# Layer 0 of a two-layer decoder step: first projections by chunks of tokens, loads and gated units moved forward

## The chip, the cores and the metric

The kernel runs on one core of a Trainium2 chip. The time is that of the device, in microseconds (us), for one execution; a kernel's figure is the median of several executions. The engines are named as the profile names them: PE (TensorE matmuls; PEld its weight loads), DVE (VectorE), ACT (ScalarE), POOL (GpSimd), SP (SyncE, which here only issues DMAs). ACT and POOL issue DMAs too, in line with their other instructions.

## The reference, cut to what matters

One step of a decoder with two layers on 1024 prompt tokens and 8 x 4 sample tokens (1056 tokens in all, width 1024). The change lies in layer 0, which is a state-space layer with two branches:

```python
proj = rms_norm(x, g) @ w_in                 # [u 512 | z 1024 | xBC 2048 | dt 16]
u, z, xbc, dt_raw = split(proj)
ya, s5_h  = s5_mixer(u, ...)                 # diagonal scan, then a gate:
    # zg = einsum('bsgc,gce->bsge', y, glu_w) + glu_b;  out = zg[..., :16] * sigmoid(zg[..., 16:])
yb, ssd_h, conv_new = ssd_mixer(z, xbc, dt_raw, ...)
x += concat(ya, yb) @ w_out
```

`rms_norm` is `x * rsqrt(mean(x*x) + 1e-5) * g` for every token. Layer 1 (attention), the two MLPs and the last norm follow; they are not touched.

## The kernel before, in words

**Tiling.** Activations lie with 128 channels on the partitions and the 1056 tokens along a row, so a 1024-wide activation is 8 tiles `x`. The tokens go in three chunks of 352 (CH). Every f32 matmul is made of three: the operand is split into a high part (`xh`, `wh`: the rounded value) and a low part (`xl`: the rest), and `xh*wh`, `xl*wh`, `xh*wl` are summed in PSUM (L381, L382, L383, in `dense`). A unit of 128 output channels has 24 such matmuls a chunk. Its 1024 x 128 weights are loaded as `wr` and split by ACT (L312) and DVE (L313) in `w_split`.

**Norm.** For each chunk ACT squares the eight `x` tiles (L418), PE multiplies them by a 128 x 128 matrix of ones (L419), so that the sum over the channels stands on all 128 partitions, and DVE and ACT turn that 128 x 352 tile into the factor `rB`: TENSOR_SCALAR (L424), square root (L425), RECIPROCAL (L426). One row of the raw sum is stored in DRAM as `msx_d` (L422, L423), from which SP later loads `m1x` in another layout (L1275, L1276). DVE scales `x` by the norm's weight and `rB` (L431), ACT makes `xh` (L432), DVE `xl` (L433).

**Order.** The tile scheduler emits one in-order stream per engine. The program gives two lists, `main` (units) and `side` (the work of the mixers), and `merge` deals the one among the other. The first units of `main` are the four `u` units (0 to 3), whose output ACT copies out of PSUM into tiles `u` (L570) and stores as `u_d` (prompt) and `us_d` (samples); then come eight `z` units and the rest. `mm`, the PSUM tile of a chunk of a unit, has four buffers. The `u` tiles take slots that tiles `x` leave free. S5 works in four batches of 8 groups: `prep` steps form the batch's matrices (`R`, stored as `rt_d` and loaded back as `Tl`, L619 and L624), `load_u` loads `U` and `Us` from `u_d` and `us_d` (L684, L686, L687), and matmuls L698, L703 and L757 use them. `s5b` and `s5x` are two parameter tiles of S5, loaded by ACT (L438, L535).

Later in the layer four `ssd_group` lists run as `side` under `conv_unit` lists. Behind the third, each of the four gated units of S5 (`load_ya`) loads a 544 KB tile `ya` from `ya_d` (L1130), forms a weight tile `glu` on DVE (L1133), multiplies (L1141), applies the gate (ACT L1143, DVE L1145), and splits the result for the eight `oa` units, which project it.

**What is touched.** `w_split` (L305), the norm loop (L402 to L433), the order of the `u` units and of the S5 batches (L807 to L812), the loop over the groups (about L1113) and `load_ya` (L1128).

```python
T.matmul(p[:, :CH], C["ones"], sq[:, :CH], start=(k == 0), stop=(k == KD - 1))   # L419
for j in range(4):
    main += u_unit(j)                                                            # unit after unit
for j in range(4):
    load_ya(j)                                                                   # ahead of the oa units
```

Of the kernel before, what the change touches and what calls it, by code (L numbers as in the profile page):

```python
# [7 lines left out]
F32 = mybir.dt.float32  # L8
# [185 lines left out]
def _build(ctx, nc, tc, ins, outs, dbg):  # L194
# [100 lines left out]

    held = {U_IO + i for i in range(3)}
    AHEAD = 300

# [6 lines left out]
    def w_split(i, al=None):  # L305
        if i < len(units) and i not in hl and i not in held:
            w_load(i)
# [95 lines left out]
    msx_d = dp.tile([1, NT], F32, name="msx_d")  # L403
    xr = [slot(F32, "x") for _ in range(KD)]
    for c in range(3):
        cc = slice(c * CH, (c + 1) * CH)
        for k in range(KD):
            nc.sync.dma_start(xr[k][:, cc], ins["xT"][k][:, cc])
            if c == 0 and k == 3:
                w_load(0)  # L410
        if c == 0:
            w_load(1)
    for c in range(3):
        cc = slice(c * CH, (c + 1) * CH)
        p = px()
        for k in range(KD):
            sq = half(F32, "sq")
            S.activation(sq[:, :CH], xr[k][:, cc], AF.Square)  # L418
            T.matmul(p[:, :CH], C["ones"], sq[:, :CH], start=(k == 0), stop=(k == KD - 1))  # L419
        rB = half(F32, "rB")[:, :CH]  # L420
        ms = half(F32, "msx")
        V.tensor_copy(ms[0:1, :CH], p[0:1, :CH])  # L422
        nc.scalar.dma_start(msx_d[:, cc], ms[0:1, :CH])  # L423
        V.tensor_scalar(rB, p[:, :CH], 1.0 / D, EPS, op0=OP.mult, op1=OP.add)  # L424
        S.activation(rB, rB, AF.Sqrt)  # L425
        V.reciprocal(rB, rB)  # L426
        if c == 0:
            w_split(0)
        for k in range(KD):
# [378 lines left out]
    for j in range(4):  # L808
        pre, run = s5_batch(j)
        side += pre + run  # L810
    for j in range(4):
        main += u_unit(j)  # L812
    m1 = main
# [105 lines left out]
    def ssd_group(g):  # L919
# [178 lines left out]
        def fin(i):  # L1098
# [5 lines left out]
            if g < 3:  # L1104
# [6 lines left out]
                F(stage_b, 3), F(stage_c, 3), F(fin, 0), F(fin, 1)]  # L1111

    for f in dt_unit(12 + SPILL):  # L1113
        f()
    side = [dt_math]
    for g in range(4):
        main = []
        for k in range(4):
            if 4 * g + k >= SPILL:
                main += conv_unit(13 + 4 * g + k, 4 * g + k)  # L1120
        merge(main, side)
        side = ssd_group(g)
# [4 lines left out]
    def load_ya(j):  # L1127

        y, o = xslot(F32, "ya"), slot(F32, "yo")
        nc.sync.dma_start(y[:, :1088].rearrange("p (t n) -> p t n", t=8), ya_d[j])  # L1130
        w = half(F32, "glu")
# [29 lines left out]

    for j in range(4):
        load_ya(j)
    main = []
    for d in range(8):
# [1357 lines left out]
```

## Time and profile before

| | |
|---|---|
| median of 3 executions | 3127.24 us (3126.2 to 3130.1) |
| the profiled execution | 3129.79 us |
| its span in the trace | 3128.0 us |
| mean granted TensorE clock | 0.978 |
| DVE, ACT, POOL busy | 70%, 45%, 21% of the span |
| DMA traffic | 414.30 MB, mean 132 GB/s |

A view of waits lists who waited for whom, the longest total first. A timeline gives the instructions of an engine in order of time, those of one form in a row merged. Each engine works in order, so an instruction that waits holds up all that stand behind it in its stream.

### The profile page before, as it was taken

To read this page: it belongs to the slowest core of one execution; us is meant where nothing else is said; L and a number is where in the kernel's file an instruction comes from. 1 tells how busy PE (TensorE), PEld (TensorE's weight loads), DVE (VectorE), ACT (ScalarE), POOL (GpSimd) and SP (SyncE) were. 2 spreads that over 40 slices of the span, in tenths; PEclk is the share of its full clock that TensorE was granted. 3 is DMA by queue.
4 is the path that set the end of the run, shared out by engine and by line. 5 is a ranking of instruction groups with operands and counts; after the bars stand their busy time and mean duration, and the time that the engine had idled before them with its cause. 6 is when DMAs were issued, how large, how long until landed. Compare 5 with 4: busy or idle time off the path is not lost. (4 is left out here: it accounts for less than half of the span.)

```text
span 3128.0 us, 58908 instructions
## 1 busy us (share of the span) xinstructions
PE 2970.6 (95%) x22228; PEld 2798.3 (89%) x22228; DVE 2204.7 (70%) x4618; ACT 1412.5 (45%) x2920; POOL 662.9 (21%) x659
## 2 busy tenths in 40 slices
PE   7999998998999999999999989999989899999998
PEld 5999886898999999999999877777869899999998
DVE  5778787778777666866223778777766877757687
ACT  4224565433333344453226666656662433334343
POOL 0000000014222001241001343434332422200133
PEclk8999999998999999999999999999999899999999
DMA  5254444522444584676532121221134344467565
GB/s 187 88 136 136 106 138 118 160 104 96 143 142 146 176 287 130 202 248 192 155 89 76 18 66 45 39 56 38 27 83 137 106 149 144 141 218 244 150 222 159
DMA packets 301285, 414.30 MB, mean 132 GB/s; under 512 B 81012, under 2 KB 202071, under 8 KB 300935
## 3 DMA queue, kind: packets, MB, share of 16 engines
q1 hardware_dynamic: 264640, 340.87, 35.8%
q0 software_dynamic: 20800, 45.43, 5.8%
q10 hardware_dynamic: 15558, 24.22, 2.1%
q8 instruction: 175, 2.87, 0.4%
q14 instruction: 112, 0.91, 0.1%
HBM read 283.81 MB, written 118.18 MB: 129 GB/s over the span
## 5 line engine op out<-in xcount | busy, mean ns | idle before, releaser
L1514 PE MATMUL dn<-xb,sb 128*128 128x264 f32 x1664 | 473.0, 287 | 2.6 <-DVE xb L1427 2.6
L1515 PE MATMUL dn<-xb,sb 128*128 128x264 f32 x1664 | 468.2, 285 | 0.0
L1513 PE MATMUL dn<-xb,sb 128*128 128x264 f32 x1664 | 455.3, 286 | 12.9 <-ACT xb L1426 10.5
L1513 PEld LDWEIGHTS dn<-xb,sb 128*128 128x128 f32 x1664 | 306.8, 189 | 13.5 <-ACT xb L1426 10.9
L1514 PEld LDWEIGHTS dn<-xb,sb 128*128 128x128 f32 x1664 | 315.1, 189 | 3.5 <-DVE xb L1427 3.4
L1515 PEld LDWEIGHTS dn<-xb,sb 128*128 128x128 f32 x1664 | 316.0, 190 | 0.0
L1372 PE MATMUL A<-xw,sw 128*128 128x264 f32 x1024 | 294.8, 289 | 15.9 <-ACT sw L1326 8.5
L1373 PE MATMUL A<-xw,sw 128*128 128x264 f32 x1024 | 294.5, 288 | 3.4 <-DVE xw L1233 3.4
L1374 PE MATMUL A<-xw,sw 128*128 128x264 f32 x1024 | 293.5, 287 | 0.0
L2243 POOL TENSOR_SCALAR P<-P,s,gates 128x640 f32<-128x640 f32 (+7 forms) x256 | 212.2, 843 | 281.0 <-DVE s L2239 231.9
L381 PE MATMUL mm<-xh,wh 128*128 128x352 f32 x672 | 225.4, 336 | 8.1 <-ACT xh L432 7.0
L382 PE MATMUL mm<-xl,wh 128*128 128x352 f32 x672 | 223.4, 333 | 5.3 <-DVE xl L433 5.2
L383 PE MATMUL mm<-xh,wh 128*128 128x352 f32 x672 | 222.6, 331 | 0.0
L2261 DVE TENSOR_TENSOR PT<-px,PT 128x512 fp32r<-128x512 f32 x264 | 177.1, 683 | 53.5 <-ACT PT L2260 52.8
L1372 PEld LDWEIGHTS A<-xw,sw 128*128 128x128 f32 x1024 | 195.6, 192 | 17.5 <-ACT sw L1326 9.0
L2285 PE MATMUL pv<-PT,vs 128*128 128x512 f32 x528 | 195.8, 439 | 11.7 <-ACT PT L2260 6.7
L1373 PEld LDWEIGHTS A<-xw,sw 128*128 128x128 f32 x1024 | 195.4, 191 | 4.1 <-DVE xw L1233 4.1
L2235 ACT ACTIVATE P<-sc,m 128x640 f32<-128x640 f32 (+7 forms) x256 | 180.1, 713 | 41.5 <-DVE m L2229 31.2
L2260 ACT CAST PT<-px 128x512 fp32r<-128x512 f32 x264 | 152.6, 594 | 98.3 <-PE px L2271 97.3
L1374 PEld LDWEIGHTS A<-xw,sw 128*128 128x128 f32 x1024 | 196.1, 192 | 0.0
L2215 PE MATMUL sc<-KT,qt 128*128 128x256 f32 x1216 | 193.6, 298 | 0.0
L2229 DVE TENSOR_REDUCE m<-sc 128x1 f32<-128x640 f32 (+7 forms) x176 | 167.0, 949 | 30.9 <-PE sc L2215 26.9
(652 smaller groups left out, 8465.6 us busy)
## 6 DMA issues: line engine op xcount, KB each, us to landing
ar<-i_w_dn SPq DMA_DIRECT2D x256, 256.0 KB
wu<-i_w_up SPq DMA_DIRECT2D x64, 512.0 KB
br<-h0t_d SPq DMA_DIRECT2D x64, 264.0 KB
wr<-i_w_in_e POOLq DMA_DIRECT2D x26, 512.0 KB, 4.5
h0t_d<-ts SPq DMA_DIRECT2D x96, 132.0 KB
br<-h0b_d SPq DMA_DIRECT2D x48, 264.0 KB
h1t_d<-ts SPq DMA_DIRECT2D x96, 132.0 KB
br<-h1b_d SPq DMA_DIRECT2D x48, 264.0 KB
```

The source lines that it names most:

```text
L381: T.matmul(o, wh, xh, start=(j == 0), stop=False)
L382: T.matmul(o, wh, xl, start=False, stop=False)
L383: T.matmul(o, wl, xh, start=False, stop=(j == n - 1))
L1372: T.matmul(o, a, xh, start=bool(first and q == 0), stop=False, skip_group_check=True)
L1373: T.matmul(o, a, xl, start=False, stop=False, skip_group_check=True)
L1374: T.matmul(o, b, xh, start=False, stop=(q == 3), skip_group_check=True)
L1513: T.matmul(o, a, h, start=(q == 0), stop=False)
L1514: T.matmul(o, a, g, start=False, stop=False)
L1515: T.matmul(o, b, h, start=False, stop=(q == 15))
L2215: T.matmul(p[:, c:c + n], w_, t, start=first, stop=True, skip_group_check=True)
L2243: nc.gpsimd.tensor_scalar(P, P, b["s"][:, h:h + 1], GT[:, qb, gc:gc + 1], op0=OP.mult, op1=OP.mult)
L2285: T.matmul(PV[g, qb, i], v, t, start=(a == 0 and kb == 0 and k == 0), stop=False)
```

## The change

Four edits, all in layer 0.

1. **The norm's factors on 88 partitions.** The tokens of a chunk are taken as 4 x 88. Each squared tile is now the stationary operand of four matmuls with one column of ones, so the sums of 88 tokens stand on 88 partitions in one column (32 matmuls a chunk instead of 8 of 352 columns). The DVE and ACT steps work on 88 x 4 elements. Four transposes with broadcast bring the result to 128 x 352, and ACT copies it to `rB`. `msx_d` is stored from 88 partitions, element by element, instead of as one row.
2. **The `u` units by chunks.** `main` begins with chunk 0 of units 0 to 3, then chunk 1, then chunk 2. The weights of units 0 and 1 are split after the norm of chunk 0, those of 2 and 3 after that of chunk 1 and in slots of another pool (`xslot`); unit 4 is held back (`nosplit`) until the last chunk.
3. **S5 loads ahead.** In each batch `load_u` stands before `prep`.
4. **Gated units among SSD work.** `ya_load` is a step of its own. The first two loads stand before the last six steps of `ssd_group(2)`, and the four `load_ya` steps are dealt among the steps of `ssd_group(3)`.

```diff
+    nosplit = {4}
...
     def w_split(i, al=None):
-        if i < len(units) and i not in hl and i not in held:
+        if i < len(units) and i not in hl and i not in held and i not in nosplit:
...
+    TT, TW = 4, 88
+    xm = const("xm", [TW, 6 * TT], own=True)
...
+    wal[2] = wal[3] = xslot
...
             S.activation(sq[:, :CH], xr[k][:, cc], AF.Square)
-            T.matmul(p[:, :CH], C["ones"], sq[:, :CH], start=(k == 0), stop=(k == KD - 1))
+            for i in range(TT):
+                T.matmul(p[:TW, i:i + 1], sq[:, i * TW:(i + 1) * TW], C["ones"][:, 0:1],
+                         start=(k == 0 and i == 0), stop=(k == KD - 1), skip_group_check=True)
+        ms, r3 = xm[:, 2 * TT * c:2 * TT * c + TT], xm[:, 2 * TT * c + TT:2 * TT * (c + 1)]
+        V.tensor_copy(ms, p[:TW, :TT])
+        nc.scalar.dma_start(msx_d[0, cc].rearrange("(i p) -> p i", p=TW), ms)
+        V.tensor_scalar(r3, ms, 1.0 / D, EPS, op0=OP.mult, op1=OP.add)
+        S.activation(r3, r3, AF.Sqrt)
+        V.reciprocal(r3, r3)
+        p = px()
+        for i in range(TT):
+            T.transpose(p[:, i * TW:(i + 1) * TW], r3[:, i:i + 1].to_broadcast([TW, 128]), ident[:TW, :TW])
         rB = half(F32, "rB")[:, :CH]
-        ms = half(F32, "msx")
-        V.tensor_copy(ms[0:1, :CH], p[0:1, :CH])
-        nc.scalar.dma_start(msx_d[:, cc], ms[0:1, :CH])
-        V.tensor_scalar(rB, p[:, :CH], 1.0 / D, EPS, op0=OP.mult, op1=OP.add)
-        S.activation(rB, rB, AF.Sqrt)
-        V.reciprocal(rB, rB)
-        if c == 0:
-            w_split(0)
+        S.copy(rB, p[:, :CH])
+        for j in range(2):
+            w_split(2 * (c > 0) + j) if c < 2 else None
...
-        side += pre + run
-    for j in range(4):
-        main += u_unit(j)
+        side += run[:1] + pre + run[1:]
+    uu = [u_unit(j) for j in range(4)]
+    for c in range(3):
+        main += [f[c] for f in uu]
+        if c == 2:
+            main.insert(-3, nosplit.clear)
+            main.insert(-2, lambda: w_split(4))
...
+    def ya_load(j):
+        YL[j] = xslot(F32, "ya")
+        nc.sync.dma_start(YL[j][:, :1088].rearrange("p (t n) -> p t n", t=8), ya_d[j])
...
+        if g == 3:
+            side = side[:-6] + [F(ya_load, 0), F(ya_load, 1)] + side[-6:]
...
-        y, o = xslot(F32, "ya"), slot(F32, "yo")
-        nc.sync.dma_start(y[:, :1088].rearrange("p (t n) -> p t n", t=8), ya_d[j])
+        if j not in YL:
+            ya_load(j)
+        y, o = YL.pop(j), slot(F32, "yo")
...
-    for j in range(4):
-        load_ya(j)
-    main = []
+    main = [F(load_ya, j) for j in range(4)]
     for d in range(8):
         main += oa_unit(d)
     merge(main, side)
```

Lines of the changed kernel are 12 to 24 higher than those of the same statement before. Here is DVE before, between chunk 1's last low parts and chunk 2's scaling (`xl` is the low part, `rB_273` chunk 2's factor):

```order
L433 TENSOR_TENSOR xl_92<-x_102,xh_91 128x352
L433 TENSOR_TENSOR xl_94<-x_103,xh_93 128x352
L523 TENSOR_SCALAR s5b_306<-s5b_306 64x512
L431 SCALAR_TENSOR_TENSOR x_96<-x_96,p_norm_mix_even,rB_273 128x352
...
L431 SCALAR_TENSOR_TENSOR x_103<-x_103,p_norm_mix_even,rB_273 128x352
L1277 TENSOR_SCALAR m1x_6125<-m1x_6125 128x9
```

And the same stretch of DVE now (`xm` holds the norm's 88 x 4 values, `rB_382` is chunk 2's factor):

```order
L445 TENSOR_TENSOR xl_80<-x_96,xh_79 128x352
L535 TENSOR_SCALAR s5b_410<-s5b_410 64x512
L445 TENSOR_TENSOR xl_82<-x_97,xh_81 128x352
...
L445 TENSOR_TENSOR xl_94<-x_103,xh_93 128x352
L429 COPY xm<-px_323 88x4
L431 TENSOR_SCALAR xm<-xm 88x4
L433 RECIPROCAL xm<-xm 88x4
L1301 TENSOR_SCALAR m1x_6213<-m1x_6213 128x9
L1289 COPY sc_6218<-m1x_6213 128x9
L365 RECIPROCAL sc_6218<-sc_6218 128x9
L692 MEMSET Us_911 64x64
L443 SCALAR_TENSOR_TENSOR x_96<-x_96,p_norm_mix_even,rB_382 128x352
```

The step on `s5b` now stands after the first low part of chunk 1 instead of after the last, the norm of chunk 2 behind all of them, and the steps on `m1x`, which need all of `msx_d`, ahead of chunk 2's scaling instead of behind it.

On ACT the first copies of the `u` units out of PSUM stand as before behind the last casts of chunk 2 and the load of `s5x`. Before, these were two chunks of unit 0 and one of unit 1:

```order
L432 CAST xh_93<-x_103 128x352
L535 DMA s5x_318<-i_s_c 128x1024
L570 COPY u_361<-mm_336 128x44x8
L570 COPY u_361<-mm_367 128x44x8
L570 COPY u_449<-mm_424 128x44x8
```

Now these are chunk 0 of all four units, and the factor of chunk 2 stands behind a step on `sc` (L364), which comes of `m1x`:

```order
L430 DMA msx_d<-xm 88x4x1
L432 ACTIVATE xm<-xm 88x4
L364 ACTIVATE sc_6218<-sc_6218 128x9
L438 COPY rB_382<-px_377 128x352
L444 CAST xh_79<-x_96 128x352
...
L444 CAST xh_93<-x_103 128x352
L547 DMA s5x_422<-i_s_c 128x1024
L582 COPY u_465<-mm_440 128x44x8
L582 COPY u_492<-mm_467 128x44x8
L582 COPY u_519<-mm_494 128x44x8
L582 COPY u_548<-mm_523 128x44x8
```

So the four buffers of `mm` hold chunk 0 of the four units until these copies run.

On SP the loads of the gated units stood behind the stores of the third group's `yb`:

```order
L1008 DMA o_ssd_p<-S_5087 128x256
L1105 DMA yb_d<-yb_4633 128x1056
L1105 DMA yb_d<-yb_4636 128x1056
L1130 DMA ya_5162<-ya_d 128x1088
L1130 DMA ya_5195<-ya_d 128x1088
L1130 DMA ya_5228<-ya_d 128x1088
L1130 DMA ya_5261<-ya_d 128x1088
```

Now two of the four stand ahead of them, and the last behind the loads of the sample states `s`:

```order
L1133 DMA ya_5074<-ya_d 128x1088
L1133 DMA ya_5076<-ya_d 128x1088
L1024 DMA o_ssd_p<-S_5179 128x256
L1121 DMA yb_d<-yb_4721 128x1056
L1121 DMA yb_d<-yb_4724 128x1056
L1133 DMA ya_5316<-ya_d 128x1088
L1056 DMA s_5351<-i_state_ssd 128x1024
L1056 DMA s_5352<-i_state_ssd 128x1024
L1133 DMA ya_5372<-ya_d 128x1088
```

In the same way the first batch's `U` loads stood on SP behind `rt_d`, the eight `Tl` loads and a store of states; they now stand directly behind the two `m1x` loads, ahead of `rt_d`.

## Rows read from the trace of the kernel before

**Rows 1.** The page's part 1, PE alone: busy us, share of the span, instructions.

```profile
PE 2970.6 (95%) x22228; PEld 2798.3 (89%) x22228; DVE 2204.7 (70%) x4618; ACT 1412.5 (45%) x2920; POOL 662.9 (21%) x659
```

**Rows 2.** Waits of PE, 0 to 110 us: total, times, longest.

```profile
PE px L419 <- ACT sq L418: 10.8, 4, 6.4
PE mm L381 <- ACT xh L432: 7.0, 2, 5.8
PE mm L382 <- DVE xl L433: 5.2, 1, 5.2
```

**Rows 3.** Timeline of DVE, 20 to 60 us: start, us, instruction, count, [idle before].

```profile
19.95 2.35 DVE L426 RECIPROCAL rB<-rB 128x352 f32<-128x352 f32 x1 [2.11 <-ACT rB L425]
...
40.86 3.49 DVE L433 TENSOR_TENSOR xl<-x,xh 128x352 fp32r<-128x352 f32 x8
51.39 0.42 DVE L523 TENSOR_SCALAR s5b<-s5b 64x512 f32<-64x512 f32 x1 [7.04 <-DMA s5b<-i_s_b]
51.73 4.04 DVE L431 SCALAR_TENSOR_TENSOR x<-x,p_norm_mix_even,rB 128x352 f32<-128x352 f32 x8
55.70 0.16 DVE L1277 TENSOR_SCALAR m1x<-m1x 128x9 f32<-128x9 f32 x1
```

**Rows 4.** Timeline of ACT and the DMAs that it issues (ACTq), 20 to 100 us.

```profile
28.84 0.34 ACTq L438 DMA_DIRECT2D s5b<-i_s_b  x1
...
34.30 0.25 ACTq L423 DMA_DIRECT2D msx_d<-msx  x1
...
56.81 1.43 ACT L570 COPY u<-mm 128x352 f32<-128x352 f32 x2 [0.52 <-DVE xl L433]
...
95.25 0.74 ACT L570 COPY u<-mm 128x320 f32<-128x320 f32 x1
```

**Rows 5.** Timeline of SP's DMA issues (SPq), 0 to 62 us.

```profile
25.56 0.89 SPq L1596 DMA_DIRECT2D o_win_s<-i_state_win  x1
49.83 0.39 SPq L1275 DMA_DIRECT2D m1x<-msx_d  x1
```

**Rows 6.** Line L343, matmuls of one column: ns min/median/max.

```profile
L343 PE MATMUL px<-csts,yacc x18: 170/250/271, 628.2 to 630.1; 128*128 128x1 f32 x16, 128*32 128x1 f32 x2
```

**Rows 7.** Stages: us, busy by engine (instructions), granted clock, DMA share, GB/s.

```profile
60.00:80.00 20.00, 20.00 (x127) 20.00 (x126) 3.43 (x5) 6.65 (x11) 1.06 (x2) 1.00 0.32 108
...
126.00:142.00 16.00, 11.40 (x57) 11.05 (x57) 12.35 (x39) 3.86 (x9) 0.00 (x0) 0.79 0.31 89
```

**Rows 8.** Waits of PE, 110 to 350 us.

```profile
PE px L703 <- DMA U<-us_d: 3.9, 1, 3.9
PE px L703 <- DMA U<-u_d: 1.6, 1, 1.6
PE px L639 <- DVE R L618: 0.7, 1, 0.7
```

**Rows 9.** Timeline of SP's DMA issues, 119 to 140 us.

```profile
125.43 3.62 SPq L624 DMA_DIRECT2D Tl<-rt_d  x8
...
129.57 4.11 SPq L684 DMA_DIRECT2D U<-u_d  x8
```

**Rows 10.** Timeline of DVE, 60 to 125 us.

```profile
84.95 0.18 DVE L471 TENSOR_TENSOR s5t<-p_s_a,s_dt 128x32 f32<-128x32 f32 x1
```

**Rows 11.** Waits of PE, 500 to 560 us.

```profile
PE px L1141 <- DMA ya<-ya_d: 9.3, 1, 9.3
```

**Rows 12.** Timeline of SP's DMA issues, 522 to 540 us.

```profile
527.21 0.81 SPq L1105 DMA_DIRECT2D yb_d<-yb  x2
528.12 3.56 SPq L1130 DMA_DIRECT2D ya<-ya_d  x4
```

**Rows 13.** Timeline of PE, 524 to 545 us.

```profile
534.82 6.55 PE L1141 MATMUL px<-ya,glu 128*128 128x408 f32 x12 [9.26 <-DMA ya<-ya_d]
542.01 2.98 PE L1141 MATMUL px<-ya,glu 128*128 128x408 f32 x8 [0.65 <-ACT sg L1143]
```

**Rows 14.** Timeline of DVE, 522 to 545 us.

```profile
525.57 0.49 DVE L1133 TENSOR_TENSOR glu<-p_s_glu,csts 128x128 f32<-128x128 f32 x2
```

More of the change, by code (lines that the diff above doesn't have):

```diff
@@ L1111, in ssd_group @@
                 F(stage_b, 3), F(stage_c, 3), F(fin, 0), F(fin, 1)]
+    YL = {}
+    def ya_load(j):
+        YL[j] = xslot(F32, "ya")
+        nc.sync.dma_start(YL[j][:, :1088].rearrange("p (t n) -> p t n", t=8), ya_d[j])
+    F = lambda f, *a: (lambda: f(*a))
     for f in dt_unit(12 + SPILL):
```

## The prediction

> **What bounds the kernel now.** I read the page's first part, then the waits of PE in three stretches, then timelines of the engines that PE waited for. PE is busy for 95% of the span [rows 1], so an edit is worth what it takes from PE's gaps and from the stretches in which PE runs at half clock behind a gap. A matmul of 352 columns takes 0.16 us of PE's time at full clock: in 60 to 80 us PE is never idle, the granted clock is 1.00, and 127 matmuls fill 20 us [rows 7]. A chunk of a unit, 24 of them, is 3.8 us.
>
> Three places with gaps are touched. At the start PE waits 10.8 us for the squares and 12.2 us for the first high and low parts [rows 2]. Behind that stands the wait of DVE for `s5b`, which ends at 51.39 us [rows 3]; that load was issued at 28.84, behind the 4 MB copy `o_win_s` of 25.56 [rows 4, 5]. In the S5 stretch PE waits 3.9 and 1.6 us for loads of `U` and 0.7 for `R` [rows 8]: SP issues the `U` loads only behind the `Tl` loads [rows 9]. At the gated units it waits 9.3 us for `ya` [rows 11], which SP issues at 528.12 behind the stores of `yb` [rows 12].
>
> **The start.** The norm on 88 partitions takes 2.35 us of reciprocal [rows 3] and the wide steps beside it away, and adds the split of two more units on DVE and ACT, four transposes and a copy in front of chunk 0's scaling. Each chunk also trades 8 matmuls of 352 columns for 32 of one column. Nine such matmuls, two records each, lie in 628.2 to 630.1 [rows 6], 0.21 us for one and 6.8 a chunk; four go with each square, and only the last four, 0.85 us, stand behind the last square of chunk 0. I take chunk 0's factor as 2 us later (bounds 1 us earlier and 4 later). What decides is behind it, since chunk 0 of all four units takes 15 us, which PE does at once, and then stands: all four `mm` buffers are full until ACT copies them out, and these copies stand behind chunk 2's casts, as in the order shown.
>
> So I follow chunk 2 from L, the landing of `s5b`. It was at 51.39. It is issued some 2 to 3 us later, and the weights of units 4 and 5 load in the same stretch, because units 2 and 3 are split earlier: 1 MB beside the 4.5 MB that took 26 us (25.56 to 51.39), so 0 to 6 us more. I take L = 55 (51.4 to 58). From L:
> - The step on `s5b` 0.34 us, seven low parts at 0.44 (3.49 for eight), 3.1 [rows 3], and the copy of the sums 0.16, as the small step L1277 [rows 3].
> - The store of `msx_d` and then the load of `m1x`, in line. This wait is new, since DVE's steps on `m1x` stand ahead of chunk 2's scaling. Behind them on DVE wait the scaling and all of S5, and on ACT, through L364, the factor, the casts and the copies of `u`. The load was issued at 49.83 and used, without a wait, at 55.70 [rows 3, 5], so it takes at most 5.9 us for 1056 elements of 4 bytes. The store writes 352 such elements where it wrote one row, so by a third of that bound 2 us. From above, the old store was issued at 34.30 and SP went on behind it only at 49.83 [rows 4, 5], up to 15.5 us; but the big copy was running then, and it should be done at L. I take 2 for the store and 3 for the load, 5 in all (2 to 21.4).
> - Three small DVE steps, L364 and the copy of the factor, with the handovers: 1.4 us.
> - Eight scalings 4.0, two low parts 0.9 [rows 3] and the first copy of `u`, 0.75 [rows 4].
>
> Sum 15.6 us, so PE starts chunk 1 at 70.6. It has eight chunks left: 30.4 us, and 2.5 for half clock behind the long gap (two such stretches cost 16 x 0.21 = 3.4 us in 126 to 142 [rows 7]). The `u` units end at 103.5. Before, the last copy of `u` began at 95.25, right behind PE [rows 4]. **Term 1: 8.3 us lost** (0 to 13 with the store as taken).
>
> The Trainium skill ("DMA: Bandwidth & Descriptors", Specifications) says that a transfer below 512 bytes is made by read-modify-write. By it the 352 elements may each cost a read more; if the store took twice as long, term 1 would be 10.3 and the time 3120. Only the changed kernel's trace can show it, since before stores one row a chunk.
>
> **The S5 stretch.** With `load_u` in front, SP issues the first batch's `U` loads as soon as `u_d` is stored, near 100 us instead of 129.57 [rows 9], and PE uses them after 130. DVE's scalars of S5 began at 84.95 [rows 10]; they now follow chunk 2's low parts, near 72, while PE is 8 us later. So `R` should not be late either. The three gaps are 6.2 us, and the half clock behind two of the stalls in 126 to 142 cost 3.4 (above), 9.6 in all. Against it: in batches 1 and 2 the loads of `U` now stand ahead of `rt_d` and `Tl` on SP; eight `U` issues take 4.1 us there [rows 9], against which DVE has gained some 20 us in the first batch. What hides this is PE's work on the `z` units; if that is used up, 1 us a batch comes back. I take **term 2: 8 us gained** (4 to 10).
>
> **The gated units.** The first two `ya` loads are issued some us before the stores of `yb`, and while they fly PE has the steps of the fourth SSD group, which stood behind the gated units before. The 9.3 us go [rows 11]. The half clock behind the gap goes too: 12 matmuls took 6.55 us, 0.55 each, and the next 8 took 2.98, 0.37 each [rows 13], so 12 x 0.17 = 2.1 us. What is late next is `glu`, on DVE at 525.57, 0.49 for two steps, behind the third group's work [rows 14]: 1 us. The third and fourth `ya` loads are still behind the `yb` stores, and the four issues took 3.56 us [rows 12]; the SSD steps between the gated units cover them, and if not, 2 to 4 us of the wait stay. **Term 3: 9.5 us gained** (6 to 11).
>
> **Sum.** 8 + 9.5 - 8.3 = 9.2 us gained on the profiled execution's 3129.79, so 3120.6. That execution is 2.55 us above the median of the runs, 3127.24; against the median the forecast is **3118 us**.
>
> **Rivals.**
> - *The start loses little.* `s5b` lands at 51.4 all the same and the pair of small DMAs takes 2 us: term 1 becomes 8.3 - 3.6 - 3 = 1.7, the time 3111. For it: the copy `o_win_s` may simply set the end, whenever `s5b` is issued. Against it: the copy itself is issued later too.
> - *The gaps come back elsewhere.* Other loads take the place of `U` (the `Tl` loads of batches 1 and 2), or the last two `ya` are late: terms 2 and 3 come to half, 8.7, and nothing is left, 3127. For it: SP is in order and the same loads only change places. Against it: DVE's earlier scalars, and the fourth SSD group as cover.
> - *Chunk 2 hangs on two small DMAs, and the kernel is slower.* The store of `msx_d` takes 15.5 us and the load of `m1x` 5.9, as at most before, since other loads run beside them. That is 16.4 more than taken, PE starts chunk 1 at 87, and the kernel loses 7.2, 3134. From a store and load of 14.2 us in all the gain is gone; from 20.5 the kernel is slower by more than 0.2%. For it: SP's long wait for `msx_d` in before. Against it: the 4 MB copy is over by then.
> - *The change does not do what it says* for the gated units, because the merge puts their steps before the loads have landed: 9 us of term 3 stay, 3127.
>
> **How the numbers follow.** Forecast 0.55, little lost at the start 0.15, gaps elsewhere 0.15, the gated units still waiting 0.05, the slower one 0.10. The forecast's own range is 3112 to 3125. With the neighbours, a start that loses nothing and both gains at their upper ends gives about 3107, and gains lost altogether 3129, so the range is 3107 to 3129; the slower rival is left out. A difference under 0.2%, 6.3 us, can't be told from none in this kernel: up to 3121 counts as faster. Faster: 0.5 of the forecast's 0.55 and the 0.15 of a cheap start, less 0.02 for luck the other way, 0.63. Same: most of the two cases of returning gaps, and what is left of the forecast, 0.25. Slower: 0.12, the last rival with a little of the others.
>
> **What would show it.** Right: DVE idle for `s5b` between chunk 1's first and second low part and for `m1x` before chunk 2's scaling; PE idle in two pieces from about 45 to 70 us, waiting for the copies of `u`; the last copy of `u` near 103 us; no wait of L715 (was L703) for `U`; no wait of L1167 (was L1141) over 2 us for `ya`; from some 650 us on the same trace, shifted. Wrong: chunk 1 starting before 62 or after 80 us; a wait of 3 us or more for `Tl` or `R` between 110 and 350 us; a gap of 5 us or more at 520 to 550.

## The result and the profile after

The kernel became slower: 3143.61 us (median of 5 runs, 3136.72 to 3145.99) against 3127.24 (5 runs on the same chip, 3123.21 to 3130.1). The ratio is 1.0051, 95% interval 1.0039 to 1.0063. The profiled execution took 3144.72 us, its span is 3142.9. Forecast was 3118.

The page's first part, all engines, answers to [rows 1]:

```profile
PE 2985.0 (95%) x22384; PEld 2820.4 (90%) x22384; DVE 2200.4 (70%) x4618; ACT 1416.3 (45%) x2927; POOL 655.0 (21%) x659
```

PE is busy 14.4 us longer than before, and the span is 14.9 us longer. PE has 156 more records. The page alone could suggest that the loss is more work and nothing else; the stages show that it is only a part. I cut both traces at the same instructions: the last copy of `u`, the first step on `S`, the last copy into `xp`, the 24th addition of the output product, the first matmul of the first MLP. "Half" is the part of PE's busy time in which the granted clock was half.

| stage | before us | after us | PE idle before, after | half before, after |
|---|---|---|---|---|
| start, to the last `u` copy | 95.8 | 112.9 | 23.1, 33.0 | 13.3, 12.0 |
| S5 stretch, to the first `S` step | 259.3 | 252.1 | 7.5, 0.0 | 17.1, 6.8 |
| to the last copy into `xp` | 170.9 | 170.0 | 5.5, 6.8 | 3.4, 12.9 |
| gated units and output product | 100.5 | 104.3 | 10.2, 7.3 | 8.8, 22.1 |
| to the first MLP matmul | 103.9 | 103.6 | 4.1, 2.0 | 0.0, 3.4 |

The differences add up to 12.6 us lost at the first MLP matmul (730.3 before, 742.9 after). The other 2.3 us of the span lie behind it, where the instructions are the same; over the fourteen profiles of this case that part takes 2390.7 to 2402.4 us, so 2.3 is within its scatter. One cut is not at the same work of PE: behind the change the first `S` step comes some 50 unit matmuls (8 us) later in PE's stream. The last copy into `xp` has nearly the same work of PE before it, so the second and third row are best read together: 430.2 us before, 422.1 after.

**The start.** Waits of PE from 0 to 110 us in the changed kernel, answering to [rows 2] (engine, line, what it waited for, total, times, longest):

```profile
PE mm L383 <- ACT u L582: 19.8, 1, 19.8
PE px L425 <- ACT sq L423: 7.6, 3, 6.5
PE px L436 <- DVE xm L433: 5.5, 1, 5.5
```

The 19.8 us are new. PE has done chunk 0 of all four units and waits for a copy of `u`. DVE's timeline says what the copies stand behind, answering to [rows 3] (start, us, instruction, count, idle before):

```profile
24.03 4.05 DVE L443 SCALAR_TENSOR_TENSOR x<-x,p_norm_mix_even,rB 128x352 f32<-128x352 f32 x8
...
43.81 0.42 DVE L535 TENSOR_SCALAR s5b<-s5b 64x512 f32<-64x512 f32 x1
...
49.58 0.17 DVE L433 RECIPROCAL xm<-xm 88x4 f32<-88x4 f32 x1 [0.43 <-ACT xm L432]
...
72.11 0.17 DVE L1301 TENSOR_SCALAR m1x<-m1x 128x9 f32<-128x9 f32 x1 [22.36 <-DMA m1x<-msx_d]
...
73.11 4.06 DVE L443 SCALAR_TENSOR_TENSOR x<-x,p_norm_mix_even,rB 128x352 f32<-128x352 f32 x8
```

There is no wait for `s5b` at all: it was used at 43.81. DVE stands for 22.36 us for `m1x`, with chunk 2's factor long formed. The DMAs of the two issuing engines, ACT first, answering to [rows 4], with the first and the last copies of `u` that followed:

```profile
31.63 0.36 ACTq L450 DMA_DIRECT2D s5b<-i_s_b  x1
...
48.98 0.31 ACTq L430 DMA_DIRECT2D msx_d<-xm  x1
...
78.07 2.68 ACT L582 COPY u<-mm 128x352 f32<-128x352 f32 x4 [0.39 <-DVE xl L445]
...
112.39 0.74 ACT L582 COPY u<-mm 128x320 f32<-128x320 f32 x1 [3.03 <-PE mm L385]
```

Then SP's issues, answering to [rows 5], and the waits of SP's queue behind them:

```profile
10.98 20.61 SPq L412 DMA_DIRECT2D x<-i_xT  x16
...
32.10 0.89 SPq L1620 DMA_DIRECT2D o_win_s<-i_state_win  x1
67.64 0.39 SPq L1299 DMA_DIRECT2D m1x<-msx_d  x1
```

```profile
SPq L1299 <- DMA msx_d<-xm: 34.5, 1, 34.5
SPq L412 <- DMA msx_d<-xm: 7.2, 1, 7.2
```

The round trip through `msx_d` is to be read here: store issued at 48.98, landed when SP goes on at 67.64 (18.7 us), values used at 72.11 (4.5 more). The second wait is a surprise. Inside the loads of `x` SP waited 7.2 us for chunk 0's store of `msx_d`, whose landing is counted on the same semaphore as one of these loads. So the 4 MB copy `o_win_s` was issued at 32.10, not at 25.56 [rows 5]. The windows in which DVE stood (busy time of PE, PEld, DVE, ACT, POOL; granted clock, DMA share, GB/s):

```profile
58.00:60.00 2.00, 1.07 (x7) 0.78 (x5) 0.00 (x0) 0.00 (x0) 0.00 (x0) 1.00 0.60 260
60.00:62.00 2.00, 0.00 (x0) 0.00 (x0) 0.00 (x0) 0.00 (x0) 0.00 (x0) 1.00 0.10 1
62.00:64.00 2.00, 0.00 (x0) 0.00 (x0) 0.00 (x0) 0.00 (x0) 0.00 (x0) 0.91 0.03 0
64.00:66.00 2.00, 0.00 (x0) 0.00 (x0) 0.00 (x0) 0.00 (x0) 0.00 (x0) 0.50 0.00 0
66.00:68.00 2.00, 0.00 (x0) 0.00 (x0) 0.00 (x0) 0.00 (x0) 0.00 (x0) 0.50 0.00 0
```

What moved until 62 us is seen by queue. By the sizes of their packets, q1 carries SP's DMAs (here the pieces of `o_win_s`, 63.5 KB each) and q10 those of ACT (here the single elements of `msx_d`). Packets, MB and share, first from 48.9 to 60.5 us, then q10 from 60.5 to 62.5:

```profile
q1 hardware_dynamic: 26, 1.69, 46.8%
q10 hardware_dynamic: 125, 0.00, 0.6%
```

```profile
q10 hardware_dynamic: 477, 0.00, 13.4%
```

The last piece of the copy ends at 62.0 us, and only from 60.5 on do most of the elements go, those of chunk 1's store (issued at 35.70) among them. So the copy was still under way, and the stores came through as it ended: by the updates of their semaphores chunk 1's store had landed at 65.97 and chunk 2's at 67.50. The last 5 us hold no packet and no work of an engine.

PE's part of the new norm from 0 to 112 us, squares and transposes, by groups (shape and count, busy us and mean ns, idle before them and what ended it):

```profile
L425 PE MATMUL px<-csts,sq 128*88 128x1 f32 x192 | 25.3, 267 | 7.6 <-ACT sq L423 7.6
...
L436 PE MATMUL px<-csts,xm 88*128 88x88 f32 x12 | 1.8, 282 | 5.5 <-DVE xm L433 5.5
```

And from PE's timeline two runs of these one-column matmuls, answering to [rows 6], and the first matmul of chunk 1:

```profile
23.72 9.55 PE L425 MATMUL px<-csts,sq 128*88 128x1 f32 x64 [0.99 <-ACT sq L423]
...
42.70 6.06 PE L425 MATMUL px<-csts,sq 128*88 128x1 f32 x64
...
78.90 0.66 PE L383 MATMUL mm<-xh,wh 128*128 128x352 f32 x1 [19.82 <-ACT u L582]
```

**The S5 stretch.** From 110 to 350 us PE waits for nothing, where [rows 8] had 6.2 us. SP's issues, answering to [rows 9]:

```profile
105.12 6.85 SPq L696 DMA_DIRECT2D U<-u_d  x8
...
131.48 3.62 SPq L636 DMA_DIRECT2D Tl<-rt_d  x8
```

**The gated units.** Waits of PE from 500 to 570 us, answering to [rows 11], and its timeline, answering to [rows 13]:

```profile
PE px L1167 <- issue: 3.6, 1, 3.6
PE px L1167 <- DVE glu L1159: 2.4, 1, 2.4
```

```profile
536.96 4.70 PE L1167 MATMUL px<-ya,glu 128*128 128x408 f32 x8 [2.35 <-DVE glu L1159]
...
546.72 5.46 PE L1167 MATMUL px<-ya,glu 128*128 128x408 f32 x8 [3.62 <-issue]
...
569.18 1.10 PE L1088 MATMUL px<-csbs,s 128*64 128x4 f32 x32
...
571.72 5.02 PE L1109 MATMUL px<-xm,ws 32*128 32x512 f32 x6
```

The 9.3 us wait for `ya` is gone, and two smaller ones stand in its place. Behind the small matmuls of the sample states (L1088, L1109), which now stand together behind the last gated unit, lies this window:

```profile
572.00:586.00 14.00, 14.00 (x37) 8.70 (x37) 10.93 (x20) 5.95 (x13) 0.20 (x1) 0.51 0.59 199
```

PE was busy for all of it, at half the clock: by an estimate, half of the stretch, 7 us more than the same work takes at full clock.

### The profile page after: what moved, and what is told of

The parts are those of the page before. It is cut to its first block, busy times and chain, and to the rows that moved or that the text cites. A ratio compares the mean times of both kernels' runs of the same rounds, so it can differ in the third digit from the quotient of the medians.

```text
span 3142.9 us, 59238 instructions
## 1 busy us (share of the span) xinstructions
PE 2985.0 (95%) x22384; PEld 2820.4 (90%) x22384; DVE 2200.4 (70%) x4618; ACT 1416.3 (45%) x2927; POOL 655.0 (21%) x659
## 5 line engine op out<-in xcount | busy, mean ns | idle before, releaser
L1537 PE MATMUL dn<-xb,sb 128*128 128x264 f32 x1664 | 456.9, 286 | 14.9 <-ACT xb L1450 11.2
L383 PE MATMUL mm<-xh,wh 128*128 128x352 f32 x624 | 210.5, 337 | 23.8 <-ACT u L582 19.8
L1396 PEld LDWEIGHTS A<-xw,sw 128*128 128x128 f32 x1024 | 196.1, 192 | 15.5 <-ACT sw L1350 8.7
L384 PE MATMUL mm<-xl,wh 128*128 128x352 f32 x624 | 207.4, 332 | 0.0
L385 PE MATMUL mm<-xh,wh 128*128 128x352 f32 x624 | 207.0, 332 | 0.0
```

What stands on the lines that cost most here:

```text
L383: T.matmul(o, wh, xh, start=(j == 0), stop=False)
L384: T.matmul(o, wh, xl, start=False, stop=False)
L385: T.matmul(o, wl, xh, start=False, stop=(j == n - 1))
L1396: T.matmul(o, a, xh, start=bool(first and q == 0), stop=False, skip_group_check=True)
L1537: T.matmul(o, a, h, start=(q == 0), stop=False)
```

## The experiments

All are variants of the changed kernel but the last, which is one of the kernel before. Ratios are to the kernel before on the same chip. "Start" is the time of the last `u` copy (95.8 before, 112.9 after).

**1. Nothing of chunk 2 behind `m1x`.** The two loads go into a scratch tile and not into a constant, so they are no longer due early.

```diff
-    V.memset(m1x, 1.0)
-    nc.sync.dma_start(m1x[:, 0:8], msx_d[0, 0:TP].rearrange("(i p) -> p i", p=128))
+    m1h = half(F32, "m1h")
+    V.memset(m1h[:, :9], 1.0)
+    nc.sync.dma_start(m1h[:, 0:8], msx_d[0, 0:TP].rearrange("(i p) -> p i", p=128))
...
-    V.tensor_scalar(m1x, m1x, 1.0 / D, 1.0, op0=OP.mult, op1=OP.add)
+    V.tensor_scalar(m1x, m1h[:, :9], 1.0 / D, 1.0, op0=OP.mult, op1=OP.add)
```

> The changed kernel, with the two m1x loads going into a tile that is only free late in the layer, so that nothing near the start waits for msx_d. The stores by elements stay. Theory 1 (the start's loss is DVE's 22 us wait for m1x): chunk 2's scaling begins near 56 us instead of 73.1, PE's chunk 1 near 62 instead of 78.9, the last copy of u near 96 instead of 112.4, the time falls by 16 to 3128 (3125 to 3131). Rival 2 (the order by chunks holds the loss, since the copies of u stand behind chunk 2's casts): chunk 1 still starts after 70 us, the time stays above 3135. Rival 3 (the stores by elements hold up the other DMAs): as theory 1, but o_win_s is still issued at 32 us, and half of the loss stays.

Measured: 3126.28 us, ratio 0.9993 (0.9977 to 1.0009). The start is 100.5, 12.4 shorter, and the loss of the change is gone in the total; that the total fell by 17 us and not by 12 is within the two intervals. Chunk 1 starts at 68.79, 10 us earlier, and not near 62 as theory 1 had it. Its DVE timeline, 40 to 75 us:

```profile
57.18 0.42 DVE L535 TENSOR_SCALAR s5b<-s5b 64x512 f32<-64x512 f32 x1 [11.28 <-DMA s5b<-i_s_b]
...
63.00 4.06 DVE L443 SCALAR_TENSOR_TENSOR x<-x,p_norm_mix_even,rB 128x352 f32<-128x352 f32 x8 [1.42 <-ACT rB L438]
```

Chunk 2's scaling starts at 63.00 and not at 73.11, though here `s5b` is late, by 11.28 us, since its load (33.31) came behind `o_win_s` (33.10). So the wait for `m1x` is shown as the costliest piece; without it, `s5b` is the next in line.

This run also prices the store without the copy. Chunk 2's store goes out behind the end of `o_win_s` (59.4 us here). Its issue, and q10 from 60.7 to 62.5 us:

```profile
60.75 0.31 ACTq L430 DMA_DIRECT2D msx_d<-xm  x1
```

```profile
q10 hardware_dynamic: 363, 0.00, 10.2%
```

All its packets moved within 1.2 us of the issue, and by its semaphore it had landed at 66.97, 6.2 us after the issue instead of 18.5. The 5 us behind the last packet are there too. So 12 of the 18.7 us were the wait for the copy, read from one profile against two: in experiment 4 the store took the same time as in the changed kernel (issued at 50.11, SP went on at 68.95; the copy ended at 63.6). No run takes the copy away and leaves the rest as it is.

**2. The mean squares stored as rows again,** by one transpose and a copy more, beside edit 1.

```diff
-        nc.scalar.dma_start(msx_d[0, cc].rearrange("(i p) -> p i", p=TW), ms)
+        pt4, m4 = px(), half(F32, "m4")
+        T.transpose(pt4[:TT, :TW], ms, ident[:TW, :TW])
+        V.tensor_copy(m4[:TT, :TW], pt4[:TT, :TW])
+        nc.scalar.dma_start(msx_d[0, cc].rearrange("(i p) -> i p", p=TW), m4[:TT, :TW])
```

> As e_late_m1x, and msx_d stored as four rows of 88 values (one more transpose and a small DVE copy a chunk) instead of 352 elements. Theory 1 alone: within 2 us of e_late_m1x. Rival 3 (the stores by elements also hold up the x loads of chunk 2, which SP issued behind a 7.2 us wait for msx_d): o_win_s issued near 26 instead of 32 us, chunk 1 starts another 4 to 6 us earlier, near 57, and the time is 3123 (3120 to 3126).

Measured: 3128.86 us, ratio 0.9999 (0.9987 to 1.0010), start 100.5 as in 1. SP's issues, 20 to 75 us:

```profile
20.16 5.17 SPq L412 DMA_DIRECT2D x<-i_xT  x7
...
27.14 0.90 SPq L1625 DMA_DIRECT2D o_win_s<-i_state_win  x1
```

SP no longer stops inside the `x` loads, and `o_win_s` goes out 6 us earlier than in 1 (33.10). So the hold came from the store of single elements. The start gains nothing by it, and the 3123 of rival 3 missed: DVE now waits 9.2 us for the transposes, which queue behind PE's other work.

**3. The norm of the kernel before,** all else as changed.

```diff
-            for i in range(TT):
-                T.matmul(p[:TW, i:i + 1], sq[:, i * TW:(i + 1) * TW], C["ones"][:, 0:1], ...)
+            T.matmul(p[:, :CH], C["ones"], sq[:, :CH], start=(k == 0), stop=(k == KD - 1))
...
+        V.tensor_scalar(rB, p[:, :CH], 1.0 / D, EPS, op0=OP.mult, op1=OP.add)
+        S.activation(rB, rB, AF.Sqrt)
+        V.reciprocal(rB, rB)
```

> The changed kernel with the norm of before (8 matmuls of 352 columns a chunk, wide reciprocal, msx_d stored as a row); the order by chunks, the S5 loads and the gated units stay. Theory 1: the m1x step now stands behind chunk 2's low parts on DVE, so the start's loss goes; chunk 1 starts before 58 us and the time is 3118 (3112 to 3126). Rival 2: chunk 1 starts after 65 us and the time is above 3130.

Measured: 3123.07 us, ratio 0.9985 (0.9976 to 0.9995); the start is 93.1 and chunk 1 starts at 58.73. Against 1 and 2 the norm on 88 partitions costs 7.4 us of the start by itself, beside what its store does to `m1x`. The matmuls of the norm in this kernel, 0 to 93 us:

```profile
L424 PE MATMUL px<-sq,csts 128*128 128x352 f32 x48 | 20.9, 593 | 12.7 <-ACT sq L423 12.7
```

PE was busy for 27.1 us with the norm in the changed kernel (25.3 and 1.8), and is for 20.9 here. Up to the last `u` copy PE is busy for 70.3 us here and for 79.5 in 1, and idle for 22.7 and 21.0.

**4. The gated units of the kernel before,** all else as changed.

```diff
-        if g == 3:
-            side = side[:-6] + [F(ya_load, 0), F(ya_load, 1)] + side[-6:]
...
-    main = [F(load_ya, j) for j in range(4)]
+    for j in range(4):
+        load_ya(j)
+    main = []
```

> The changed kernel with the gated units as before (loads behind the yb stores, units ahead of the merge); all else stays. From the traces, the stretch from the last xp copy to 651 us was 125.2 us before and 128.5 in the changed kernel. Theory (dealing the gated units among the SSD steps costs 3 us: less gap, but more half clock and a longer DVE and ACT chain): the time falls by 3 to 3140 (3137 to 3143). Rival (the move gains the 9.5 us forecast, and something else lost as much): the time rises to 3153.

Measured: 3139.82 us, ratio 1.0036 (1.0025 to 1.0046). A gap of 10.4 us for `ya` is back, and yet the gated stage is shorter (102.4 against 104.3), with 10.1 us at half clock in place of 22.1. Moving the units among the SSD work gained nothing here; the two ratios, 1.0036 and 1.0051, have intervals that overlap.

**5. Experiment 3 with `s5b` issued first,** by SP right behind `x`, and with edit 1.

```diff
+    b_raw = slot(F32, "s5b")
+    nc.sync.dma_start(b_raw[:, :1024], ins["s5_b"])
     for c in range(3):
...
-    b_raw = slot(F32, "s5b")
-    nc.scalar.dma_start(b_raw[:, :1024], ins["s5_b"])
```

> The kernel of e_old_norm (the changed kernel with the norm of before), with s5b loaded by SP right behind the x loads, ahead of the 4 MB copy o_win_s, and the m1x loads late as in e_late_m1x. In e_old_norm PE waited 10.0 us for the copies of u, which stood behind DVE's 3.6 us wait for s5b (until 56.3 us). Theory 1 (with the waits for small DMAs gone, the order by chunks has PE busy from chunk 0 on): PE starts chunk 1 near 53 us instead of 58.7, the last copy of u is near 87 instead of 93.1, the time 3117 (3112 to 3121) against 3123. Rival (the copies of u wait for chunk 2's casts and low parts whatever the DMAs do): chunk 1 starts after 57 us, the time stays at 3122 or more.

Measured: 3114.49 us, ratio 0.9960 (0.9943 to 0.9977); the start is 88.9. First SP's issues, then PE's first matmul of chunk 1 (78.90 in the changed kernel):

```profile
27.53 0.98 SPq L419 DMA_DIRECT2D s5b<-i_s_b  x1
...
29.03 0.89 SPq L1614 DMA_DIRECT2D o_win_s<-i_state_win  x1
```

```profile
55.61 0.66 PE L383 MATMUL mm<-xh,wh 128*128 128x352 f32 x1 [7.56 <-ACT u L575]
```

**6. Experiment 3 without the order by chunks:** one unit behind the other, the early `U` loads kept.

```diff
-    for c in range(3):
-        main += [f[c] for f in uu]
...
+    nosplit.clear()
+    for j in range(4):
+        main += u_unit(j)
```

> The kernel of e_old_norm with the u units one after the other as before: of the change only the S5 loads and the gated units are left. Theory: the last copy of u is at 95.8 us as in before; the S5 stretch (from there to the first S step of SSD) takes 252 us, as in the changed kernel, against 259.3 before; the gated stretch (last xp copy to the end of the oa units) costs 2 us more than before. Together 5 us faster than before: 3123. If the S5 stretch is short only because DVE starts earlier in the order by chunks, it stays at 257 or more and the time is 3128 or more.

Measured: 3131.35 us, ratio 1.0008 (0.9997 to 1.0018). The start is 92.9, as in 3, but the S5 stretch is 259.7, as long as before. SP's first issues of `U`, then PE's waits, 80 to 350 us:

```profile
66.29 3.84 SPq L689 DMA_DIRECT2D U<-u_d  x8
```

```profile
PE px L708 <- DMA U<-us_d: 2.7, 1, 2.7
```

The first `U` loads go out at 66 us, and PE's idle time in the stretch falls from 7.5 to 3.8 us. But at the last copy into `xp`, where PE's work is level, nothing is gained: 430.0 us from the last `u` copy, against 430.2 before and 422.3 in 3. So the forecast of 3123 missed, and the early loads alone are not what shortens it. The start is no longer than in 3, so the order by chunks brings nothing there.

**7 and 8. `glu` formed early.** Beside the norm of before, the two DVE steps on `glu` stand at the load of `ya`; in 7 the gated units are a block again behind two early loads, in 8 they are dealt out as changed.

```diff
     def ya_load(j):
+        GL[j] = w = half(F32, "glu")
+        for h in range(2):
+            V.tensor_tensor(w[:, h * 128:(h + 1) * 128]..., glut[...], C["gmask"][...], OP.mult)
...
+        w = GL.pop(j)
```

> The kernel of e_old_norm, with the first two ya loads and their glu tiles early, and the four gated units again ahead of the merge, as a block. Theory (in the changed kernel the dealt steps cost more in half clock, by sample-state matmuls in one run, and in waits for glu than the early loads give): the stretch from the last xp copy to the end of the oa units, 124.4 us before and 126.7 in e_old_norm, falls to 117, and the time to 3114 (3110 to 3119). Rival (DVE and ACT set the gated units' pace, so the early loads give little in any order): the stretch stays over 122 us, the time over 3119.

> The kernel of e_old_norm, with the glu tiles formed with the ya loads; the gated units stay dealt among the SSD steps. Theory as in f_block_glu: the waits of 2.4 and 4.0 us before the first and second unit shrink to 3 us together, but PE still runs 10 us or more at half clock behind the sample-state matmuls, so the stretch is 123 us (121 to 125) and the time 3120. Rival (the waits for glu are all that is wrong): the stretch is under 119 us and the time 3115.

Measured: 7: 3121.14 us, ratio 0.9967 (0.9955 to 0.9979); 8: 3122.59, 0.9978 (0.9968 to 0.9987). Both lie within 2 us of 3, with intervals that overlap, and the gated stage is no shorter (103.2 and 102.5 us, 102.5 in 3): the 3114 of 7 missed. PE's longest wait, 480 to 570 us, of 8:

```profile
PE px L1161 <- ACT sg L1163: 4.6, 3, 3.4
```

The wait for `glu` is gone and PE waits for the sigmoid of the unit before it (L1163). The wait moved.

**9, 10 and 11. The gated units on the base of 5.** In 9 they stand as before (the edit of 4). In 10 they are dealt out as changed, and the fourth group's sample-state steps are spread over its list; 11 is 10 with `glu` early.

```diff
+        if g == 3:
+            return [F(load_xc), start, F(stage_a, 0), F(stage_a, 1), F(stage_b, 0), F(stage_c, 0), F(samp_a), F(stage_a, 2),
+                    F(stage_b, 1), F(samp_b), ysm, F(stage_c, 1), F(samp_c, 0), F(stage_a, 3), F(stage_b, 2), F(stage_c, 2),
+                    F(samp_c, 1), F(stage_b, 3), F(stage_c, 3), F(fin, 0), F(fin, 1)]
         return [F(load_xc), F(samp_a), F(samp_b), F(samp_c, 0), F(samp_c, 1), start, ...
```

> The kernel of f_s5b with the gated units as before (loads behind the yb stores, units ahead of the merge). In f_s5b the stretch from the first S step of SSD to the MLP's first A matmul takes 371.7 us, before it took 375.2. Theory (moving the gated units trades idle time for half clock and gives nothing that can be told): PE idle in that stretch rises by 4 us, its half-clock busy time falls by 5 to 10, the stretch is 372 to 376 us and the time is 3116, within 4 us of f_s5b's 3114.5. Rival (the early loads are worth their 9 us, which the half clock only hid in the changed kernel): the time rises to 3122 or more.

> The kernel of f_s5b, with the sample-state steps of the fourth SSD group (64 matmuls of 4 columns and their neighbours) spread among the later oa units instead of standing together behind the gated units. Theory (PE's half clock behind 543.8 us, 10.2 us in f_s5b and 13.7 at 572.2 in the changed kernel, comes of these matmuls standing together): half-clock busy time in the stretch falls from 25.0 to 16 us or less, the stretch by 4 us, the time to 3111. Rival (the half clock comes of the gated units' own waits): half-clock busy time stays over 22 us and the time at 3114 or more.

> As g_spread, and the glu tiles formed with the ya loads. Theory: the waits for glu (2.4 and 2.9 us in f_s5b's gated units) go as well, the time is 3108 (3104 to 3113). Rival (DVE and ACT set the pace there, so that the wait only moves): within 2 us of g_spread.

Measured: 9: 3118.58 us, ratio 0.9972 (0.9962 to 0.9982). 10: 3114.55, 0.9952 (0.9939 to 0.9965). 11: 3114.61, 0.9956 (0.9940 to 0.9971). PE's wait in 9:

```profile
PE px L1158 <- DMA ya<-ya_d: 11.6, 1, 11.6
```

The windows at the 4-column matmuls of the sample states and behind them. In 5 these stand at 539.8 to 542.4 us, in 10 at 576.0 to 578.5, with the 32-row ones further down:

```profile
540.00:554.00 14.00, 14.00 (x100) 9.24 (x99) 11.26 (x21) 7.11 (x13) 0.49 (x1) 0.64 0.91 341
```

```profile
576.00:579.00 3.00, 3.00 (x81) 2.88 (x82) 1.52 (x2) 0.00 (x0) 0.03 (x1) 1.00 0.31 93
579.00:583.00 4.00, 4.00 (x34) 3.67 (x31) 3.68 (x9) 1.40 (x5) 0.00 (x0) 0.57 0.00 0
```

Behind them PE runs at half clock for 10.3 us in 5 (543.8 to 554.1) and for 3.4 in 10 (579.3 to 582.7). But PE's idle time in the gated stage rises (8.4 us against 6.4), and the half-clock time of the whole stretch that the expectation names is 26.8 us against 25.0 in 5, not 16: it came back elsewhere, and the total is that of 5. So the rival of 10 came true in both its numbers, and the rival of 11 in its. In 9 half-clock time did not fall as forecast (27.8 us). From 9 to 10 the times fall by 4 us, of the 9.5 that were forecast for term 3, and the intervals just touch; from 9 to 5 they overlap.

**12. The kernel before with `s5b` issued first,** the edit of 5 alone.

> The kernel before, with one edit: the load of s5b is issued by SP directly behind the loads of x, ahead of the copy o_win_s, instead of by ACT behind chunk 0's norm. Nothing is left out. Theory (the order by chunks and the early s5b are worth something only together, because with a unit's three chunks in line PE has only 3.8 us of work between two chunks' splits): DVE's wait of 7.0 us for s5b goes, the splits of chunks 1 and 2 come some 7 us earlier, and PE's two waits behind chunk 0 (5.8 and 5.2 us) shrink by 5 to 7 us, so that the last u copy is near 90 us as in f_s5b (88.9); but the loads of U, which the early s5b does not move, keep the S5 stretch at 259, and the time is near 3122, ratio 0.998. Rival (the early s5b alone is the whole of f_s5b's gain, the rest of the change is worth nothing): 3114, ratio 0.996 or less. Second rival (s5b was no bound of the start in before): the last u copy stays within 2 us of 95.3, the time within 0.1% of before.

Measured: 3121.21 us, ratio 0.9985 (0.9974 to 0.9996). Start 89.5, S5 stretch 260.0. The last large `u` copy, at 95.25 in [rows 4]:

```profile
89.00 0.74 ACT L570 COPY u<-mm 128x320 f32<-128x320 f32 x1
```

One load put in front of a 4 MB copy gives nearly the whole start of 5 (88.9) without any order by chunks; in the total it is 0.15%. What 5 has beyond it is the S5 stretch (252.6).

This run also warns of reading one profile's clock. Its gated units stand as before, with the sample-state matmuls spaced as before, and still it has a long stretch at half clock, where the kernel before has 3.4 us (567.5 to 570.9):

```profile
556.00:570.00 14.00, 14.00 (x72) 10.93 (x72) 8.53 (x17) 3.06 (x9) 0.54 (x1) 0.52 0.96 321
```

Its gated stage takes 103.9 us. Over the profiles with this old order (before, 4, 9 and 12) the stage takes 100.5 to 103.9 us, and with the units dealt out as changed (the changed kernel, 1, 2, 3, 5, 6 and 8) 99.5 to 104.3.

## Why the prediction was wrong

**Where it failed.** The forecast had 8.3 lost and 17.5 gained. Measured, in the stages: 17.1 lost at the start, 7.2 gained in the S5 stretch, 3.8 lost at the gated units, and 1.1 gained between: 12.6 lost. Two terms failed, term 3 by 13.3 us (its 3.8 lost can't be told from none, see below) and term 1 by 8.8.

**Term 1, the start: the store and load of `msx_d`.** The steps in front were close: chunk 0's factor is 1.7 us late (scaling at 24.03; before, the reciprocal ended at 19.95 + 2.35 [rows 3]; taken 2), and `s5b` was issued at 31.63 (taken 31 to 32). L was wrong, on the good side: `s5b` had landed by 43.81, before the 51.4 that I gave as the earliest. The reason is in the order of issue: `s5b` used to stand behind `o_win_s`, now it stood ahead of it by 0.5 us. That holds in all fourteen profiles: in the seven with `s5b` behind the copy DVE used it within 2.3 us of the copy's end, in the seven with it ahead 17 us or more before that end. From `s5b` to the store it took 1.6 us more than counted, because DVE waited 1.5 for chunk 2's sums. Then comes the step that failed, "I take 2 for the store and 3 for the load, 5 in all". It took 23.1 us (48.98 to 72.11), above even the upper bound of 21.4. What stands behind it was right again: 1.0 us to the scaling (1.4), 5.8 from there to PE's chunk 1 (5.65). My reason for 2 us was that the large copy "should be done at L". But the landing of `s5b` no longer marked the end of the copy: chunk 0's store held SP, so `o_win_s` slid by 6.5 us and ran to 62.0, while L moved the other way. The store stood behind the copy; with the copy done it took 6.2 us (experiment 1), still three times the 2 that I took. The slower rival had this mechanism, priced at 16.4 us, and I gave it 0.10; the forecast took the case in which nothing else is under way. The row spoke for the rival: chunk 2's store in the trace of before, a row and not single elements, had kept SP for up to 15.5 us beside the same copy [rows 4, 5].

Experiment 1 shows the step's share: 12.4 us of the start. The norm on 88 partitions is 7.4 more, by experiment 3. Together that is 19.8 and not 17.1, because the start without both is 93.1, 2.7 better than before; experiment 6 has the same 2.7 or so without the order by chunks, and where it comes from was not tried. I had costed the norm at 2 us, at chunk 0 alone, and let the matmuls of the other chunks change places at no cost: "6.8 a chunk" is 20.4 us for three. They took 25.3, and the transposes 1.8, which I had named for chunk 0 only, against 20.9 in experiment 3. That is 6.2 us more work of PE, most of the 7.4; how much of it lay under waits was not tried.

The Trainium skill ("DMA: Bandwidth & Descriptors", Specifications) says that transfers below 512 bytes are made by read-modify-write; by it I had given 2 us more. The trace shows when the store landed, not a read. Most of its 18.7 us it stood behind the copy, and the last 5 hold no packet, so no run here shows such reads.

**Term 2, S5: right in size, wrong in cause.** 7.2 us came of 8 in the stretch, 8.1 up to the last copy into `xp`, and all waits of [rows 8] went. I put it down to the early `U` loads and the early scalars. Experiment 6 has these loads at 66 us and gains nothing; experiment 3, which differs by the order by chunks alone, has 251.6. So the order by chunks is needed for it, and that the size fits is luck as far as my reason goes. Whether it would do alone, with the loads as before, was not tried.

**Term 3, the gated units: nothing gained.** "The 9.3 us go" held, and `glu` was late next, as said: 2.4 us and not 1, and a second wait of 3.6 that I had not named. So idle time fell only from 10.2 to 7.3. What failed is "the half clock behind the gap goes too": PE's work at half clock behind the gap, 5.4 us before (534.8 to 540.2), became 3.4 and 5.0 behind the two smaller waits. And 13.7 us of it lie behind the sample-state matmuls (572.2 to 585.9), where the profile of before has 3.4. Term 3 took for granted that work dealt out differently runs at the speed that it had. Is the place of these matmuls the cause? In part, at most. In the seven profiles with the units dealt out as changed the stretch behind them is 10.2 to 13.7 us, in 10 and 11, where they are spread, 3.4. But with large matmuls of the output product between them, as before, it is 3.4 in two profiles (before and 9) and 13.6 in two others (7 and 12). So what is shown is that term 3 brought nothing: over these profiles the stage is neither shorter nor clearly longer with the units dealt out than without (ranges at experiment 12). Experiments 7, 8 and 11 moved waits from DVE to ACT.

**The rivals.** "The kernel is slower" was the right one in sign and in its place, but its 3134 lacks term 3. "The gaps come back elsewhere" was right of the gated units, though not for its reason (late loads), and wrong of S5. "Does not do what it says" was wrong: the `ya` loads land in time.

**What stays open.** Why a store of single elements lands 5 us after its last packet, with the copy before it and without. Whether a store by rows would have spared the changed kernel the wait: experiment 2 takes the wait away as well. What in the order by chunks shortens the S5 stretch. What sets the half clock in the gated stage, and which part of its remaining waits comes from ACT.

**The best version** is 10, level with 5 and 11: the change without its norm, with `s5b` ahead of `o_win_s`, `m1x` off the early path and the sample-state steps spread, 0.9952 (0.9939 to 0.9965).

## What to carry to other kernels

Where a change makes one instruction wait for a DMA's landing, take the price from the nearest row of the same DMA, however unlike the surroundings seem, and ask which other transfers it will now stand behind: those may move too. Ask when each large copy ends, and not only when it was issued. Look for a small load that stands behind a large copy on which nothing waits; putting one load first shortened the start by 6 us here, nearly as much as the new order of the units brought in the S5 stretch (8 us). A gap that is filled with other work is worth only what that work costs in its new place: price its clock there, not where it stood, and look at more than one profile before a stretch at half clock is put down to an edit.

## What the runs showed of the hardware

- A store of 352 single elements, 1.4 KB from 88 partitions, landed 18.7 us after its issue beside a 4 MB copy that ended at 62.0 us, and 6.2 us after its issue when the copy had ended before it (experiment 1). In both the landing came 5 us after the last packet. The two loads behind it, 4.1 KB in all, were used 4.5 us after the first one's issue.
- A 512 KB load issued behind the 4 MB copy was used within 2.3 us of the copy's end in all seven profiles with that order; issued ahead of the copy, 17 us or more before that end in the other seven.
- Such a store at 19.53 us kept SP, which loads other data, from going on for 7.2 us; one of these loads counts on the same semaphore. With stores by rows (experiment 2) the wait was not there.
- A one-column matmul with 88 stationary columns took 0.30 us a pair of records in one run of 32 (9.55 us) and 0.19 in another (6.06).
- The granted clock was 0.51 from 572 to 586 us, the 1.2 GHz level, while PE's records fill the stretch (14.00 of 14.00 us). What PE did before was matmuls of 4 columns (L1088) and the first of those with 32 rows (L1109). The Trainium skill ("TensorE: Matmul & The Clock Gate", Why this matters for your kernels) warns of gaps between bursts of matmuls in which TensorE idles; here the records of the stretch show no gap, and the longest in the 12 us before it is 0.58 us. With the same matmuls spread (experiment 10) 3.4 us at half clock followed them, but with the order of before 3.4 in one profile and 13.6 in another (experiment 12).
